# Second norm of a hybrid encoder layer: its weight moved to ScalarE behind the store, its 1/rms applied four row blocks at a time

## The chip, the cores and the metric

The kernel runs on one core of one Trainium2 chip. The metric is the device time of one execution in microseconds (us), as a median over runs. Engines are named as the profile names them: PE (TensorE matmul), PEld (its weight loads), DVE (VectorE), ACT (ScalarE), POOL (GpSimd) and SP (SyncE, which issues the DMAs). A name with a q, as SPq, is an engine's instruction queue.

## What is computed

One layer of an encoder, for 1024 frames of a new stream and 64 frames of a running one, 1088 columns together, with 1024 features. The part that matters here lies between the mixer and the feed-forward network (FFN):

```python
def _rmsnorm(x, g):
    xf = x.astype(jnp.float32)
    y = xf * lax.rsqrt(jnp.mean(xf * xf, axis=-1, keepdims=True) + EPS)
    return (y * g.astype(jnp.float32)).astype(x.dtype)

    mix = jnp.concatenate([y.astype(h.dtype), pool_out.astype(h.dtype)], axis=-1) @ w_out
    h = h + _rmsnorm(mix, post_mix_g)
    hn = _rmsnorm(h, pre_ffn_g)
    f = (jax.nn.silu(hn @ w_gate) * (hn @ w_up)) @ w_down
    h = h + _rmsnorm(f, post_ffn_g)
```

The third line is the first norm with its residual, the fourth is the second norm, with the weight `pre_ffn_g`. The value `h` of the third line is needed again in the last one, so the kernel stores it.

## The kernel before

Features lie on the 128 partitions, columns on the free axis. The 1088 columns are four chunks of 272, and the 1024 features are eight row blocks of 128, so an activation of a chunk is eight blocks of 128x272. Two tiles of four row blocks each (`mixf` for kh = 0 and 1, 128x1088) hold the mixer's output of a chunk. Products are made from high and low parts in three matmuls: ScalarE rounds a tile to its high part (`form`, a CAST, L1477) and VectorE subtracts it from the tile for the low part (`sub`, L416). Pool and VectorE additions that may disturb each other are marked "E" in the planner.

Every piece of work is a generator that yields which engine it wants and how long the planner assumes it to take; a planner (`Layout`) runs these generators against assumed times for all engines and so writes down, once, the instruction order of every engine. On the chip each engine runs its own list in order and waits on semaphores, so a late instruction holds back everything behind it in its list. All DMAs are issued from SP, in order.

`post_mix(c)` handles a chunk after the product with `w_out`. The column sums of squares of the mixer's output (name m0 to m3 for the chunks) go through `rstd_job`: PE sums over the partitions (L527, eight matmuls of one column in the trace), VectorE makes 1/rms in nine small operations (tile `t_m`, L532 to L561), PE transposes and spreads it into a PSUM bank (L565). Then `two(i)` handles four pairs of row blocks: VectorE multiplies the pair by 1/rms (L1422), Pool adds the residual `x` (L1431, `XM` names the engine per pair), the sum is the new `h`. After two pairs, four row blocks of `h` are stored with one DMA of 544 KB (`h_dram`). `SumSq` squares the pair on ScalarE (L617), sums the squares on VectorE (L624, L635) and starts the second norm (names h0 to h3): again `rstd_job` with its matmuls on PE, tile `t_h`, and then `norm(m)` for each of eight row blocks: one SCALAR_TENSOR_TENSOR on VectorE (L1457) that multiplies by the weight column and by 1/rms.

The FFN runs per pair of chunks, p = 0 for chunks 0 and 1, p = 1 for chunks 2 and 3. It uses seven products of combined operands, as Strassen's scheme does. `hforms(p)` makes the operands from the normed tiles: forms B11 and B21 from the first chunk alone, T1 to T4 from differences (L1489) and B22. A form is ready when its high part (ACT L1477) and its low part (DVE L416) are. The products of p = 0 are the first work of the FFN on PE; those of p = 1 follow while its last forms are still being made. A product's result can also wait for a partial sum in PSUM that VectorE has to take first (L1685, flag "x1").

Beside this, `w_pp` products (L492, a projection used much later) fill PE while the statistics of chunks 2 and 3 are worked out; ScalarE copies each result out of PSUM (tile `e`, L1825). At the start of the kernel, sums of squares of the input's first chunk are added by Pool (`XE`, tile `acc_x`, L772).

Of the kernel before, what the change touches and what calls it, by code (L numbers as in the profile page):

```python
# [14 lines left out]
P = 128  # L15
# [16 lines left out]
SEQ_IN = '4567pppp'  # L32
NZ = 3

XM, XF, XP = 'GGGG', 'GDGD', 'GDDD'
XE = ('AG', 'AD', 'AD', 'AD')

XL = 'GPGD'
NWARM, LW = 5, 256
# [16 lines left out]
P_DT = 3  # L56
P_DTE = 1
P_DTC = 4

FAST_M, FAST_H = (3,), (3,)  # L60

# [6 lines left out]
NK = 8  # L68
# [147 lines left out]
class Layout:  # L216
# [20 lines left out]
    def spawn(self, gen, prio=5):  # L237
        self.seq += 1
        job = {"gen": gen, "prio": (prio, self.seq), "t": max(self.now, self.done), "eng": "P", "req": None, "ready": 0.0}
        if self.step(job):  # L240
            self.jobs.append(job)
            self.jobs.sort(key=lambda j: j["prio"])
# [93 lines left out]
def trunk(ctx, tc, xT, par, wmix, wdt, poolw, wout, wff, wdn, wpg, wpp, pT, ssm0,  # L336
# [55 lines left out]
    def dma(dst, src, cols):  # L392
        sy.dma_start(dst, src)
        return lay.load(cols)
# [9 lines left out]
    def pcol(name, i=None, n=1):  # L404
        a, b = _PCOLS[name]
        if i is None:
            return cp[:, a:b]
        return cp[:, a + i:a + i + n]
# [996 lines left out]
    def post_mix(c, mf, ss):  # L1405

        L = CH[c][1]
        flag = []
        used = [0]
        added = [0, 0]  # L1410
        ss2 = SumSq(f"h{c}", 4, lambda: spawn(second(), 0), P_SQH)

        def two(i):
            if XM[i] != "A":
                yield n2.ok
                xr = n2.take(f"xr{c}_{i}")
                yield ("S", 0, 0)
                at = dma(xr, xT[c][:, 2 * i:2 * i + 2], 2 * L)
            yield lambda: bool(flag)
            v = mf[i // 2][:, i % 2 * 2:i % 2 * 2 + 2, :]  # L1420
            yield ("D", 0.72, 0)
            ve.tensor_tensor(v, v, flag[0][:, :L].unsqueeze(1).broadcast_to([P, 2, L]), ALU.mult)  # L1422
            used[0] += 1
            if used[0] == 4:
                banks.give(flag[0])
            if XM[i] == "A":
                yield ("S", 0, 0)
                yield ("S", 0, dma_add(v, xT[c][:, 2 * i:2 * i + 2], 2 * L))
            elif XM[i] == "G":
                yield ("G", 1.35, at)  # L1430
                gp.tensor_tensor(v, v, xr, ALU.add)  # L1431
            else:
                yield ("E", 0.73, at)
                ve.tensor_tensor(v, v, xr, ALU.add)
            if XM[i] != "A":
                n2.give(xr)
            added[i // 2] += 1
            if added[i // 2] == 2:
                dma(h1_d[c][:, i // 2 * 4:i // 2 * 4 + 4], mf[i // 2], 4 * L)
            ss2.add(v)  # L1440

        for i in range(4):
            spawn(two(i), 0)
        yield from rstd_job(ss.halves(), L, 1024.0, f"m{c}", flag, fast=c in FAST_M, free=ss.free)

        def second():
            got = []
            yield from rstd_job(ss2.halves(), L, 1024.0, f"h{c}", got, fast=c in FAST_H, free=ss2.free)
            r2 = got[0]
            left = [NK, 4, 4]  # L1450
            for m in range(NK):
                spawn(norm(m, r2, left), 0)

        def norm(m, r2, left):
            v = mf[m // 4][:, m % 4, :]
            yield ("D", 0.49, 0)
            ve.scalar_tensor_tensor(v, v, pcol("pre_ffn_g", m), r2[:, :L], ALU.mult, ALU.mult)  # L1457
            left[0] -= 1
            left[1 + m // 4] -= 1
            if not left[1 + m // 4]:  # L1460
                normed.add((c, m // 4))
            if not left[0]:
                banks.give(r2)

# [907 lines left out]
```

## Time and profile before

| | us |
|---|---|
| median of 3 runs | 1226.35 (1225.46 to 1226.62) |
| the profiled execution, its own time | 1227.99 |
| span in that profile | 1226.2 |
| PE busy in the span | 1201.8 (98%) |
| VectorE busy | 862.6 (70%) |
| ScalarE busy | 577.0 (47%) |
| GpSimd busy | 65.2 (5%) |

The profile is one execution taken by the hardware profiler. Busy time is an average over stages: the stage of this change covers about 315 to 424 us of the span. "Idle before" in a row names how long the engine had stood idle and what released it. PEclk, or the granted clock, is TensorE's clock as a share of its full 2.4 GHz.

### The profile page before, as it was taken

Reading aid. Unit: us, or ns where it says so; the run is one execution under the profiler, and the core shown is the slowest. Engines: PE = TensorE matmul, PEld = TensorE weight load, DVE = VectorE, ACT = ScalarE, POOL = GpSimd, SP = SyncE. Lnnn points to the kernel's source line nnn. Section 1 sums busy time; section 2 is a strip of 40 time slices with the busy share of each in tenths; the row PEclk is TensorE's granted clock in tenths of the full one; section 3 lists DMA queues with packets and bytes.
Section 4 is the critical chain, followed back from the end, with each engine's and each line's share of the span. In section 5 each row is a group of like instructions: output and inputs, shape, how many; then the busy total and the mean of one; then the engine's idle time right before and its main releaser. Section 6 shows DMA issues by size and latency. Waiting matters only on the chain.

```text
span 1226.2 us, 23743 instructions
## 1 busy us (share of the span) xinstructions
PE 1201.8 (98%) x9641; PEld 1181.8 (96%) x9641; DVE 862.6 (70%) x1572; ACT 577.0 (47%) x1123; POOL 65.2 (5%) x56
## 2 busy tenths in 40 slices
PE   8999999999999899999999999999999999999997
PEld 6999999999999899999999999999999999988996
DVE  5796867775798786776667667766746556688765
ACT  6354657964457444443444444443432212346543
POOL 2000000111241000000000000000000000002011
PEclk8999999999999899999999999999999999999998
DMA  6122122143446044444344334337978676334422
GB/s 226 42 74 80 62 96 92 52 133 114 135 161 225 14 137 148 153 153 133 134 162 145 130 138 163 132 122 263 404 280 291 213 254 231 115 96 132 142 74 83
DMA packets 73201, 182.01 MB, mean 148 GB/s; under 512 B 8636, under 2 KB 16644, under 8 KB 73092
## 3 DMA queue, kind: packets, MB, share of 16 engines
q1 hardware_dynamic: 73092, 180.50, 42.7%
q8 instruction: 75, 1.23, 0.4%
q14 instruction: 34, 0.28, 0.1%
HBM read 121.75 MB, written 58.72 MB: 147 GB/s over the span
## 4 chain that ended last, share of the span: by engine, by line
PE 92%; DVE 3%; ACT 2%; DMA 1%; issue 1%; SPq 0%; DVEq 0%; ACTq 0%
PE psall L1642 55%; PE psall L492 29%; PE psall L509 2%; PE psall L527 1%; PE psall L1128 1%; PE psall L565 1%; PE psall L1157 1%; PE psall L1122 1%; DVE f L1905 0%; DMA raw_in<-in_wmix_dram 0%; PE psall L1243 0%; PE psall L736 0%; DMA raw_out<-in_wout_dram 0%; DVE w_out L416 0%; DMA raw_pg<-in_wpg_dram 0%
## 5 line engine op out<-in xcount | busy, mean ns | idle before, releaser
L492 PE MATMUL psall<-x,w_in 128*128 128x272 f32 x1440 | 193.7, 291 | 0.0
L492 PEld LDWEIGHTS psall<-x,w_in 128*128 128x128 f32 x1440 | 184.0, 188 | 3.3 <-issue 2.8
L1905 DVE TENSOR_TENSOR f<-f,psall 128x544 f32<-128x544 f32 (+1 forms) x96 | 60.4, 636 | 68.8 <-PE psall L1642 67.0
L1642 PE MATMUL psall<-h_T,w_g_S 128*128 128x272 f32 x792 | 104.4, 292 | 3.2 <-DVE h_T L416 2.9
L1642 PEld LDWEIGHTS psall<-h_T,w_g_S 128*128 128x128 f32 x792 | 102.5, 193 | 3.6 <-DVE h_T L416 3.1
L1642 PE MATMUL psall<-al_T,w_d_S 128*128 128x272 f32 x768 | 100.4, 289 | 1.4 <-DVE f L1905 0.9
L1642 PE MATMUL psall<-h_T,w_u_S 128*128 128x272 f32 x792 | 100.8, 287 | 0.0
L1642 PEld LDWEIGHTS psall<-al_T,w_d_S 128*128 128x128 f32 x768 | 97.7, 188 | 2.3 <-ACT w_pg L463 0.9
L1642 PEld LDWEIGHTS psall<-h_T,w_u_S 128*128 128x128 f32 x792 | 99.6, 188 | 0.0
L492 PE MATMUL psall<-mix,w_out 128*128 128x272 f32 x720 | 93.5, 289 | 0.0
L492 PEld LDWEIGHTS psall<-mix,w_out 128*128 128x128 f32 x720 | 90.9, 188 | 0.0
L1642 PE MATMUL psall<-al_B,w_d_A 128*128 128x272 f32 x528 | 72.3, 289 | 2.7 <-DVE w_d_A L416 2.6
L492 PE MATMUL psall<-h,w_pg 128*128 128x272 f32 x576 | 74.7, 289 | 0.0
L492 PEld LDWEIGHTS psall<-h,w_pg 128*128 128x128 f32 x576 | 72.8, 188 | 0.0
L1642 PEld LDWEIGHTS psall<-al_B,w_d_A 128*128 128x128 f32 x528 | 68.5, 188 | 3.3 <-DVE w_d_A L416 3.1
L1642 PE MATMUL psall<-h_B,w_g_A 128*128 128x272 f32 x528 | 69.9, 288 | 0.0
L1642 PE MATMUL psall<-h_B,w_u_A 128*128 128x272 f32 x528 | 69.8, 288 | 0.0
L1642 PEld LDWEIGHTS psall<-h_B,w_u_A 128*128 128x128 f32 x528 | 67.7, 188 | 0.0
L1642 PEld LDWEIGHTS psall<-h_B,w_g_A 128*128 128x128 f32 x528 | 67.6, 188 | 0.0
L1570 ACT CAST w_d_A<-raw_d 128x512 fp32r<-128x512 f32 (+3 forms) x44 | 22.3, 522 | 70.2 <-PE psall L1642 35.1
L1570 ACT CAST w_d_S<-raw_d 128x512 fp32r<-128x512 f32 (+3 forms) x54 | 26.5, 532 | 56.4 <-DVE raw_d L1594 33.8
L416 DVE TENSOR_TENSOR w_u_S<-raw_u,w_u_S 128x512 fp32r<-128x512 f32 x44 | 30.3, 688 | 26.5 <-ACT w_u_S L1570 26.4
(407 smaller groups left out, 2211.7 us busy)
## 6 DMA issues: line engine op xcount, KB each, us to landing
af_dram<-a_T SPq DMA_DIRECT2D x88, 272.0 KB, 2.2
al_T<-af_dram SPq DMA_DIRECT2D x44, 544.0 KB, 6.1
af_dram<-a_B SPq DMA_DIRECT2D x66, 272.0 KB, 2.7
al_B<-af_dram SPq DMA_DIRECT2D x33, 544.0 KB, 6.4
raw_g<-in_wff_dram SPq DMA_DIRECT2D x22, 512.0 KB, 3.8
raw_u<-in_wff_dram SPq DMA_DIRECT2D x22, 512.0 KB, 3.7
raw_in<-in_wmix_dram SPq DMA_DIRECT2D x15, 512.0 KB, 3.8
raw_d<-in_wdn_dram SPq DMA_DIRECT2D x14, 512.0 KB, 4.6
```

Source lines behind the costliest of these rows:

```text
L416: eng.tensor_tensor(lo, src, hi.bitcast(F32), ALU.subtract)
L492: pe.matmul(out, lhsT, rhs, start=i == 0, stop=i == n - 1)
L509: pe.matmul(out, w.v(wi, k), act.v(xi, k, L), start=first and n == 0, stop=not left and n == 2)
L527: pe.matmul(ps[:n, 500 + 4 * i + j:501 + 4 * i + j], acc[:, n * j:n * j + n], ones[:, 0:1], start=True, stop=True)
L565: pe.transpose(pss[i][:, n * j:n * j + n], y[:, 4 * i + j:4 * i + j + 1].broadcast_to([n, P]), ident[:n, :n])
L1122: pe.matmul(py[:L, 256 * g:256 * g + 256], ct[:, g, t0:t0 + L], state[:, 256 * g:256 * g + 256], start=True, stop=True)
L1128: pe.matmul(pst[:, 256 * g:256 * g + 256], bk[:L, 128 * g:128 * g + 128], xw[:L, 4 * g:4 * g + 4].rearrange("p h q -> p (h q)"), start=Tru ...
L1157: pe.matmul(pyt[64 * r:64 * r + 64, P * b:P * b + L], xdt[:L, h], es[h // 4][:L, h % 4, :L], start=first, stop=True, skip_group_check=True)
L1570: ac.copy(v[:, 0], src)
L1642: pe.matmul(d[:, p - q.ps[0], :], w.v(wi, k), u.b(bf, xi, p, k), start=start and not k and not wi and not xi, stop=k == u.ks - 1 and wi == ...
L1905: ve.tensor_tensor(v[:, sl], v[:, sl], src[:, pl], ALU.add)
```

## The change

Four things change. (1) The weight is no longer part of `norm`: after a pair of row blocks has been stored and squared, ScalarE multiplies it in place by its weight column (new `scale`, two activations of 128x272 per pair). It must wait for the store, which reads the same rows, to have landed. (2) `norm` handles four row blocks at once with one TENSOR_TENSOR of 128x1088, whose second operand is the 1/rms in PSUM, read four times. It waits until both pairs of its tile are scaled. (3) `h` is stored per pair, in 16 DMAs of 272 KB, where there were 8 of 544 KB. (4) Two tables move additions from Pool to VectorE: the fourth pair's residual (`XM`) and the first chunk's sums of squares at the start (`XE`).

```diff
@@ -32,8 +32,8 @@
 SEQ_IN = '4567pppp'
 NZ = 3
 
-XM, XF, XP = 'GGGG', 'GDGD', 'GDDD'
-XE = ('AG', 'AD', 'AD', 'AD')
+XM, XF, XP = 'GGGD', 'GDGD', 'GDDD'
+XE = ('AD', 'AD', 'AD', 'AD')
 
 XL = 'GPGD'
 NWARM, LW = 5, 256
@@ -56,6 +56,7 @@
 P_DT = 3
 P_DTE = 1
 P_DTC = 4
+P_SCL = 0
 
 FAST_M, FAST_H = (3,), (3,)
 
@@ -1407,7 +1408,7 @@
         L = CH[c][1]
         flag = []
         used = [0]
-        added = [0, 0]
+        scaled = [0, 0]
         ss2 = SumSq(f"h{c}", 4, lambda: spawn(second(), 0), P_SQH)
 
         def two(i):
@@ -1434,10 +1435,15 @@
                 ve.tensor_tensor(v, v, xr, ALU.add)
             if XM[i] != "A":
                 n2.give(xr)
-            added[i // 2] += 1
-            if added[i // 2] == 2:
-                dma(h1_d[c][:, i // 2 * 4:i // 2 * 4 + 4], mf[i // 2], 4 * L)
-            ss2.add(v)
+            at = dma(h1_d[c][:, 2 * i:2 * i + 2], v, 2 * L)
+            ss2.add(v, lambda: spawn(scale(i, v, at), P_SCL))
+
+        def scale(i, v, at):
+
+            for q in range(2):
+                yield ("A", 0.48, at)
+                ac.activation(v[:, q], v[:, q], AF.Identity, scale=pcol("pre_ffn_g", 2 * i + q))
+            scaled[i // 2] += 1
 
         for i in range(4):
             spawn(two(i), 0)
@@ -1447,18 +1453,16 @@
             got = []
             yield from rstd_job(ss2.halves(), L, 1024.0, f"h{c}", got, fast=c in FAST_H, free=ss2.free)
             r2 = got[0]
-            left = [NK, 4, 4]
-            for m in range(NK):
-                spawn(norm(m, r2, left), 0)
-
-        def norm(m, r2, left):
-            v = mf[m // 4][:, m % 4, :]
-            yield ("D", 0.49, 0)
-            ve.scalar_tensor_tensor(v, v, pcol("pre_ffn_g", m), r2[:, :L], ALU.mult, ALU.mult)
+            left = [2]
+            for h in range(2):
+                spawn(norm(h, r2, left), 0)
+
+        def norm(h, r2, left):
+            yield lambda: scaled[h] == 2
+            yield ("D", 1.27, 0)
+            ve.tensor_tensor(mf[h], mf[h], r2[:, :L].unsqueeze(1).broadcast_to([P, 4, L]), ALU.mult)
             left[0] -= 1
-            left[1 + m // 4] -= 1
-            if not left[1 + m // 4]:
-                normed.add((c, m // 4))
+            normed.add((c, h))
             if not left[0]:
                 banks.give(r2)
```

Line numbers of the changed kernel are one higher from L59 on and four to six higher behind `post_mix`: L1457 becomes L1463, L1489 L1493, L416 L417, L527 L528, L1685 L1689, L1825 L1829; the new activation is L1445. Tile names carry running numbers that differ between the kernels.

VectorE's list behind the last 1/rms of chunk 3 (`t_h`), before; `mixf_0_3521` and `mixf_1_3522` are the halves of chunk 3, `h_T_1` rows make low parts of T forms, L1685 raises the flag x1:

```order
L561 SCALAR_TENSOR_TENSOR t_h_4837<-t_h_4837 68x4
L1457 SCALAR_TENSOR_TENSOR mixf_0_3521<-mixf_0_3521,cp,psall 128x272 x4
L1489 TENSOR_TENSOR mixf_0_3519<-mixf_0_3521,mixf_0_3519 128x1088
L1457 SCALAR_TENSOR_TENSOR mixf_1_3522<-mixf_1_3522,cp,psall 128x272 x4
L1685 TENSOR_TENSOR xr_2_3903<-xr_2_3903,psall 128x272
L416 TENSOR_TENSOR h_T_1_4913<-mixf_0_3519,h_T_0_4912 128x1088
L1489 TENSOR_TENSOR mixf_0_3519<-mixf_1_3522,mixf_0_3519 128x1088
L1693 TENSOR_TENSOR sq_m_3536<-sq_m_3536,psall 128x272
L1693 TENSOR_TENSOR p_3811<-p_3811,psall 128x272
L416 TENSOR_TENSOR w_u_A_4917<-raw_u_1_4655,w_u_A_4917 128x512
L1489 TENSOR_TENSOR mixf_0_3521<-mixf_1_3522,mixf_0_3521 128x1088
L416 TENSOR_TENSOR h_T_1_4952<-mixf_0_3519,h_T_0_4951 128x1088
```

The same place after:

```order
L1463 TENSOR_TENSOR mixf_0_3521<-mixf_0_3521,psall 128x1088
L1493 TENSOR_TENSOR mixf_0_3519<-mixf_0_3521,mixf_0_3519 128x1088
L1463 TENSOR_TENSOR mixf_1_3522<-mixf_1_3522,psall 128x1088
L417 TENSOR_TENSOR w_u_A_4836<-raw_u_0_4828,w_u_A_4836 128x512
L417 TENSOR_TENSOR h_T_1_4898<-mixf_0_3519,h_T_0_4897 128x1088
L1493 TENSOR_TENSOR mixf_0_3519<-mixf_1_3522,mixf_0_3519 128x1088
L1689 TENSOR_TENSOR p_3813<-p_3813,psall 128x272
L417 TENSOR_TENSOR w_u_A_4903<-raw_u_0_4828,w_u_A_4903 128x512
L417 TENSOR_TENSOR w_u_A_4911<-raw_u_1_4829,w_u_A_4911 128x512
L1493 TENSOR_TENSOR mixf_0_3521<-mixf_1_3522,mixf_0_3521 128x1088
L417 TENSOR_TENSOR h_T_1_4948<-mixf_0_3519,h_T_0_4947 128x1088
```

Two instructions stand in the place of eight, and the flag (L1689) now stands behind the low part of T1, the difference for T2 and one weight's low part.

ScalarE's list while the squares of chunk 3 are made, before; `e` copies free PSUM banks of the `w_pp` products, L617 squares the four pairs:

```order
L617 ACTIVATE p_3811<-mixf_0_3521 128x544
L1825 COPY e_7_4709<-psall 128x272
L1825 COPY e_0_4718<-psall 128x272
L617 ACTIVATE sq_m_3273<-mixf_0_3521 128x544
L1477 CAST h_B_0_4734<-mixf_0_3519 128x1088
L617 ACTIVATE sq_m_3273<-mixf_1_3522 128x544
L1825 COPY e_1_4732<-psall 128x272
L1477 CAST h_B_0_4766<-mixf_1_3520 128x1088
L1825 COPY e_2_4743<-psall 128x272
L617 ACTIVATE xr_2_3903<-mixf_1_3522 128x544
```

After:

```order
L618 ACTIVATE sq_m_3536<-mixf_0_3521 128x544
L1829 COPY e_6_4716<-psall 128x272
L1829 COPY e_7_4725<-psall 128x272
L618 ACTIVATE sq_m_3273<-mixf_0_3521 128x544
L1829 COPY e_0_4737<-psall 128x272
L1445 ACTIVATE mixf_0_3521<-mixf_0_3521,cp 128x272 x2
L618 ACTIVATE xr_2_3681<-mixf_1_3522 128x544
L1445 ACTIVATE mixf_0_3521<-mixf_0_3521,cp 128x272 x2
L618 ACTIVATE xr_2_3681<-mixf_1_3522 128x544
L1829 COPY e_1_4748<-psall 128x272
L1829 COPY e_2_4758<-psall 128x272
L1445 ACTIVATE mixf_1_3522<-mixf_1_3522,cp 128x272 x2
```

The scales of the first two pairs now stand between the squares of the last two, and the copies `e_1` and `e_2` behind both.

PE's list around the statistics of h2, before (`w_pp0` and `w_pp1` are the two halves of the weight; this is the second pass over `w_pp0`):

```order
L492 MATMUL psall_72<-p0_0_3802,w_pp0_3806 128x272 x2
L492 MATMUL psall_72<-p0_1_3805,w_pp0_3806 128x272
L527 MATMUL psall_72<-cp_73,p0_3811 68x1 x4
L492 MATMUL psall_72<-p0_1_3805,w_pp0_3806 128x272
L492 MATMUL psall_72<-p0_0_3802,w_pp0_3807 128x272 x2
```

After, in the first pass over `w_pp1`:

```order
L493 MATMUL psall_72<-p0_0_3804,w_pp0_3809 128x272 x2
L493 MATMUL psall_72<-p0_0_3804,w_pp1_3810 128x272 x2
L493 MATMUL psall_72<-p0_1_3807,w_pp1_3810 128x272
L528 MATMUL psall_72<-cp_73,sq_m0_3273 68x1 x4
L493 MATMUL psall_72<-p0_1_3807,w_pp1_3810 128x272
L493 MATMUL psall_72<-p0_0_3804,w_pp1_3811 128x272 x2
```

The statistics of h2 come after 27 matmuls of `w_pp`, where they came after 69. In the same way the statistics of h3 come after 18 matmuls of the FFN, where they came after 33, and the transposes of `t_h` of chunk 3 after 36, where they came after 57. The transposes of `t_m` of chunk 2 stand 12 matmuls earlier than before, those of chunk 3 15 matmuls earlier.

## Rows read from the trace of the kernel before

**Rows 1.** Page, busy time, share of the span and instructions of each engine.

```profile
PE 1201.8 (98%) x9641; PEld 1181.8 (96%) x9641; DVE 862.6 (70%) x1572; ACT 577.0 (47%) x1123; POOL 65.2 (5%) x56
```

**Rows 2.** Busy time by stretch, with PEclk, DMA share and GB/s at the end.

```profile
360.00:380.00 20.00, 20.00 (x166) 20.00 (x165) 19.86 (x21) 13.84 (x26) 7.71 (x4) 1.00 0.48 173
...
408.00:414.00 6.00, 3.68 (x25) 3.26 (x25) 5.39 (x10) 3.17 (x6) 0.00 (x0) 1.00 0.00 0
414.00:416.00 2.00, 0.00 (x0) 0.00 (x0) 2.00 (x2) 0.78 (x1) 0.00 (x0) 0.88 0.00 0
416.00:424.00 8.00, 7.56 (x39) 7.56 (x40) 5.88 (x6) 2.94 (x5) 0.00 (x0) 0.60 0.00 0
```

**Rows 3.** Timeline of PE, 396 to 424: start, duration, operation, count, idle before.

```profile
396.27 3.18 PE L1642 MATMUL psall<-h_B,w_g_A 128*128 128x272 f32 x24
...
400.41 0.60 PE L527 MATMUL psall<-cp,p 128*68 128x1 f32 x8
...
403.96 0.40 PE L565 MATMUL psall<-cp,t_h 68*128 68x68 f32 x4
...
409.54 1.79 PE L1642 MATMUL psall<-h_B,w_g_S 128*128 128x272 f32 x12 [1.74 <-DVE xr L1685]
...
413.20 0.39 PE L1642 MATMUL psall<-h_T,w_g_S 128*128 128x272 f32 x1 [0.37 <-ACT h_T L1477]
416.44 7.29 PE L1642 MATMUL psall<-h_T,w_g_S 128*128 128x272 f32 x35 [2.85 <-DVE h_T L416]
```

**Rows 4.** Timeline of DVE, 396 to 424, from the last 1/rms on.

```profile
404.46 1.72 DVE L1457 SCALAR_TENSOR_TENSOR mixf<-mixf,cp,psall 128x272 f32<-128x272 f32 x4 [1.23 <-PE psall L565]
406.22 1.29 DVE L1489 TENSOR_TENSOR mixf<-mixf,mixf 128x1088 f32<-128x1088 f32 x1
407.43 1.72 DVE L1457 SCALAR_TENSOR_TENSOR mixf<-mixf,cp,psall 128x272 f32<-128x272 f32 x4
409.06 0.43 DVE L1685 TENSOR_TENSOR xr<-xr,psall 128x272 f32<-128x272 f32 x1
409.41 1.28 DVE L416 TENSOR_TENSOR h_T<-mixf,h_T 128x1088 fp32r<-128x1088 f32 x1
...
413.30 0.69 DVE L416 TENSOR_TENSOR w_u_A<-raw_u,w_u_A 128x512 fp32r<-128x512 f32 x1
415.11 1.28 DVE L416 TENSOR_TENSOR h_T<-mixf,h_T 128x1088 fp32r<-128x1088 f32 x1
```

**Rows 5.** Instructions by line and form: count, duration in ns min/median/max.

```profile
L1422 DVE TENSOR_TENSOR mixf<-mixf,psall x16: 709/713/721, 315.9 to 390.2; 128x544 f32<-128x544 f32 x16
```

```profile
L1431 POOL TENSOR_TENSOR mixf<-mixf,xr x10: 1359/1378/2408, 319.4 to 393.1; 128x544 f32<-128x544 f32 x10
```

**Rows 6.** Timeline of ACT: eight activations of 128x272 in place with a weight column.

```profile
1097.49 3.40 ACT L2081 ACTIVATE f<-f,cp 128x272 f32<-128x272 f32 x8
```

**Rows 7.** DMA issues: bytes, median us from issue to landing.

```profile
h_dram<-mixf SPq DMA_DIRECT2D x8, 544.0 KB, 2.8
```

```profile
af_dram<-a_T SPq DMA_DIRECT2D x88, 272.0 KB, 2.2
```

**Rows 8.** Timelines of PE and DVE: the statistics of h2, and the last sum before.

```profile
379.13 0.60 PE L527 MATMUL psall<-cp,p 128*68 128x1 f32 x8
```

```profile
377.08 0.43 DVE L635 TENSOR_TENSOR p<-p 128x272 f32<-128x272 f32 x1
```

**Rows 9.** Timeline of DVE: the last sum before the statistics of h3.

```profile
398.83 0.43 DVE L635 TENSOR_TENSOR p<-p 128x272 f32<-128x272 f32 x1
```

**Rows 10.** Timelines of DVE and POOL: sums of squares beside residual additions.

```profile
318.46 3.34 DVE L624 TENSOR_TENSOR sq_m<-sq_m 128x544 f32<-128x544 f32 x2
```

```profile
319.36 3.67 POOL L1431 TENSOR_TENSOR mixf<-mixf,xr 128x544 f32<-128x544 f32 x2
```

**Rows 11.** Timelines of POOL and DVE at the start.

```profile
11.52 6.92 POOL L772 TENSOR_TENSOR acc_x<-acc_x,sqx 128x272 f32<-128x272 f32 x6 [0.45 <-ACT sqx L768]
```

```profile
14.62 0.34 DVE L858 TENSOR_TENSOR cp<-cp 128x4 f32<-128x4 f32 x1 [2.13 <-DMA cp<-in_par_dram]
```

## The prediction

> **What bounds the kernel now.** The page's table of busy time comes first: PE is busy for 1201.8 of 1226.2 us [rows 1], so only the 24.4 us in which it idles, and the time in which it runs below full speed, can be won by a change that takes no matmul away. This change takes none away. The table by stretch then shows where such time lies near the change. From 408 to 414 PE works 3.68 of 6 us, from 414 to 416 not at all, and from 416 to 424 it is busy again but at a granted clock of 0.60 [rows 2]. This is the beginning of the FFN.
>
> PE's timeline of that place names the waits: 1.74 us before the row at 409.54, on the sum for the flag x1 (VectorE L1685); 0.37 before 413.20, on the high part of T2; 2.85 before 416.44, on the low part of T2 (VectorE L416) [rows 3]. Together 4.96 us. The row at 396.27 has 24 matmuls in 3.18 us, 0.1325 each. The 35 matmuls from 416.44 would take 4.64 at that pace and took 7.29, so 2.65 us are lost to the clock, which fell while PE idled: 0.88 in the 2 us in which it does nothing, 0.60 behind that. The other two waits, of 1.74 and 0.37, left it at 1.00 [rows 2, 3]. The place costs 4.96 + 2.65 = **7.61 us**.
>
> VectorE's timeline says why the flag and T2 are late. It does not idle there: from 404.46 on it runs the second norm of chunk 3 in two runs of four, with a difference between them, then the flag's sum at 409.06, the low part of T1, and the low part of T2 at 415.11 [rows 4]. All of it hangs on the transposes of 1/rms at 403.96 [rows 3], and the first norm starts 0.50 after them. So two things decide: when the last 1/rms comes, and what VectorE runs between it and the two results.
>
> **The norm itself.** A run of four takes 404.46 to 406.22, 1.76 us; a 128x1088 subtraction from SBUF takes 1.29 alone, and starts 1.21 before its successor [rows 4]. The merged multiply, with its second operand in PSUM, is not in this trace. Below stands the 1.29 of that subtraction; above stand two 128x544 multiplies from PSUM, 2 x 0.713 = 1.43 [rows 5]. It is nearest to the 128x1088 subtraction, so I take 1.21 from start to start, which saves 0.55 per half and 1.1 on the way to T2 (0.7 at the other end).
>
> **The order behind it.** The transposes of the last 1/rms now come 21 matmuls earlier in the FFN, 21 x 0.1325 = 2.78 us: at 401.2 in the time of the trace of before, if the statistics are ready. Then, going down the new list of VectorE with the starts of [rows 4]: first half at 401.7, difference 402.9, second half 404.1, low part of a weight 405.3 (0.60 from 413.30 to 413.90, where the next subtraction begins; taken as 0.60), low part of T1 405.9, difference for T2 407.1, flag 408.3, done at 408.75. PE wants the flag at 409.54 - 1.74 = 407.80. It waits 0.95, where it waited 1.74, because the flag was moved behind three instructions. Then two weights (1.2), a difference (1.21), and the low part of T2 ends about 412.4. PE, which passes the flag 0.8 earlier, wants it at 413.20 - 0.37 - 0.8 + 0.39 = 412.4. So the 2.85 us wait goes, and with it, as no wait above 1.74 is left, the low clock. What is left is 0.95 of 7.61: a gain of **6.66**. With 1.43 for each multiply the flag waits 0.4 longer.
>
> **What the earlier statistics cost.** PE's list is in order, so a statistic that is put earlier and isn't ready stops everything behind it.
> - h2: its matmuls move 42 matmuls ahead, 5.57 us. The last sum before them ended at 377.51 and PE took them at 379.13, a slack of 1.62 [rows 8]. The sums must come 3.95 earlier. The transposes that start this chain are 12 matmuls earlier, 1.6. VectorE is busy for 19.86 of 20 us there, beside 7.71 of Pool [rows 2]; the change shortens a chunk's norm by 1.1 and adds one residual addition of some 0.72, a gain of 0.4. Two sums beside two Pool additions took 3.34, where such sums alone are about as long as the 0.713 of L1422, 1.43 [rows 5, 10]: each Pool addition costs VectorE about 0.95, and there is one fewer. 1.6 + 0.4 + 0.95 = 2.95, so PE waits 1.0. Ends: 0, and 2.35 if only the transposes come earlier.
> - h3: 15 matmuls, 2.0 us, against a slack of 400.41 - 399.26 = 1.15 [rows 3, 9], and its transposes are 15 matmuls earlier as well. One Pool addition (1.38 [rows 5]) leaves its chain; four scales in front of the last square enter it, 4 x 0.43 (eight take 3.40 [rows 6]) = 1.7. I put 0.3, with ends 0 and 2.0 (all of the shift lost).
>
> **The scales and stores.** 32 scales at 0.43 add 13.6 us to ScalarE, which has 6.16 idle in 360 to 380 [rows 2]. Each first waits for its store to land. The nearest rows are 2.8 us for 544 KB and 2.2 for 272 KB [rows 7]; I take 2.2. Behind the waiting scale are the squares of later pairs and the `e` copies, on which PE's banks hang. The squares are in the line above; for the copies I put 0.3 (0 to 1.5). SP issues eight more stores, all in this stage: no engine but ScalarE waits for one before the norms do. The Trainium skill ("DMA: Bandwidth & Descriptors", section "Anatomy of one DMA — SWDGE (gpsimd) path") holds that about 2.0 us of a DMA are fixed, whatever its size; 2.2 against 2.8 for half the bytes agrees, though these are issued by SP. By its fit a 272 KB store takes some 2.6 us (an estimate), which would add 0.4 at most to the copies.
>
> **The start.** Seven additions go from Pool, where six took 6.92, to VectorE, at about the 0.43 of L1685: 3.0 us. VectorE idled 2.13 us before 14.62, waiting for a DMA that its new list no longer puts there [rows 4, 11]. I put 0, from -0.5 to +0.7.
>
> **Sum.** -6.66 + 1.0 + 0.3 + 0.3 = -5.06. From the profiled execution's 1227.99 that gives 1222.93; it lies 1.64 above the median of 1226.35, so the forecast is **1221.3**.
>
> **Rivals.**
> - *All is absorbed.* No new waits, the flag too in time: the whole 7.61, 1218.7. For it: the statistics' chains also lose a Pool addition. Against it: the flag's own walk leaves 0.95.
> - *The second result stays late.* The last 1/rms comes only 0.7 earlier instead of 2.78: then the flag waits about as before, T2 about 1.3 to 2, and the clock falls again. What remains is 0.55 per half, 1.1, less 1.0 for h2: 1226.3. For it: VectorE's list is in order and the flag now stands three instructions deeper.
> - *The store's landing becomes the bound.* SP's list is in order; a store behind a load that still waits for its buffer is issued late, and the scale then holds ScalarE, its squares and the copies. With all the upper ends, 2.35 + 2.0 + 1.5 = 5.85, and one of these waits as long as the 2.85 that came before the low clock, another 2.65: -6.66 + 5.85 + 2.65 = +1.84, 1228.2, slower by 0.15%; with the second result late as well, +1.84 + 2.85 = +4.7, 1231. It decides from a landing of about 4 us on.
> - *Pool and VectorE block each other.* Two sums beside two Pool additions took 3.34 [rows 10], and the moved fourth addition now runs beside Pool's third. If it waits for all of it, 1.38 more in the chains of h2 and h3, 2.1 together after h3's slack: 1223.4. The Trainium skill ("SBUF — State Buffer", section "Who interferes with whom") says that a VectorE instruction with two SBUF inputs and a GpSimd one that reads SBUF exclude each other for a whole instruction. The 3.34 is between no blocking (1.43) and two whole waits (4.2), so the trace bears it out in part.
>
> **Chances.** 0.45 for the forecast, 0.08 for all absorbed, 0.12 for the blocking, 0.18 for a late second result, 0.17 for the landing. A measurement of this kernel tells about 0.2%, 2.45 us, from no change: faster is below 1223.9, slower above 1228.8. The first three are faster, but for some of the blocking (0.62); the second result late is the same, with that rest and a quarter of the landing (0.25); the rest of the landing is slower (0.13). The range reaches from the first rival to where the landing begins, 1218.5 to 1228.2.
>
> **What would show it.** In the profile after: the transposes of the last 1/rms 36 matmuls into the FFN; no PE wait above 1.5 us from 400 to 425, and a granted clock of 1.00 throughout; a merged norm of 1.2 to 1.45; PE waits on VectorE at the statistics of h2 of about 1; store landings of 2.0 to 2.8. The forecast is wrong if ScalarE waits on DMAs while PE waits on ScalarE between 315 and 400, or if a wait of over 2 us before T2 is left.

## The result: 0.6% faster

The changed kernel takes 1220.20 us, median of 5 runs (1219.06 to 1222.34), where the kernel before, run beside it on the same chip, took 1226.62 (1225.46 to 1230.02). The ratio is 0.9943, with a 95% interval from 0.9924 to 0.9962. The forecast was 1221.3 in a range from 1218.5 to 1228.2. The profiled execution after took 1222.34 us with a span of 1220.6; before, 1227.99 and 1226.2. The spans differ by 5.6 us, and that is the difference that can be looked up in the two traces.

Busy time hardly moved, as the page after shows (engine, busy us, share, instructions); PE's answers to [rows 1]:

```profile
PE 1199.7 (98%) x9641; PEld 1180.5 (97%) x9641; DVE 862.8 (71%) x1559; ACT 587.8 (48%) x1155; POOL 51.0 (4%) x45
```

VectorE's total is what it was (862.6 before): it runs the 11 additions that Pool lost and a shorter norm. The gain is in PE's waits. PE's timeline after at the beginning of the FFN, which answers to [rows 3]:

```profile
402.08 0.40 PE L566 MATMUL psall<-cp,t_h 68*128 68x68 f32 x4
...
409.92 1.77 PE L1646 MATMUL psall<-h_B,w_g_S 128*128 128x272 f32 x12 [1.36 <-DVE p L1689]
411.53 1.67 PE L1646 MATMUL psall<-h_B,w_g_A 128*128 128x272 f32 x12
413.04 0.29 PE L1646 MATMUL psall<-h_T,w_g_S 128*128 128x272 f32 x1
413.53 4.74 PE L1646 MATMUL psall<-h_T,w_g_S 128*128 128x272 f32 x35 [0.20 <-DVE h_T L417]
```

The waits of 1.74, 0.37 and 2.85 have become 1.36, nothing and 0.20, and the 35 matmuls that took 7.29 take 4.74. The table by stretch after (columns as in [rows 2], granted clock third from the end) has the clock at 1.00 in every stretch, also where it was 0.88 and 0.60:

```profile
360.00:380.00 20.00, 20.00 (x165) 20.00 (x165) 19.69 (x29) 17.95 (x37) 3.51 (x2) 1.00 0.48 165
...
408.00:414.00 6.00, 4.43 (x33) 3.99 (x32) 5.96 (x8) 2.93 (x4) 0.00 (x0) 1.00 0.00 0
414.00:416.00 2.00, 2.00 (x18) 2.00 (x17) 2.00 (x4) 0.78 (x2) 0.00 (x0) 1.00 0.00 0
416.00:424.00 8.00, 8.00 (x65) 7.97 (x64) 5.64 (x8) 4.85 (x10) 0.00 (x0) 1.00 0.01 2
```

One stretch serves as a ruler below: from the transposes of m0, where the two orders still agree, to the first matmul with `w_u`, behind the waits. Its two ends on PE, before and after:

```profile
315.49 0.40 PE L565 MATMUL psall<-cp,t_m 68*128 68x68 f32 x4
...
423.57 1.68 PE L1642 MATMUL psall<-h_B,w_u_A 128*128 128x272 f32 x12
```

```profile
315.54 0.40 PE L566 MATMUL psall<-cp,t_m 68*128 68x68 f32 x4
...
418.11 2.18 PE L1646 MATMUL psall<-h_B,w_u_A 128*128 128x272 f32 x16
```

The stretch fell from 108.08 to 102.57, by 5.51 us: the whole difference of the spans. It splits at the end of the last wait. Up to there PE gained 416.44 - 413.53 + 0.05 = 2.96, behind it 7.13 - 4.58 = 2.55, the low clock.

VectorE's timeline after shows the way to T2; it answers to [rows 4]:

```profile
402.58 1.29 DVE L1463 TENSOR_TENSOR mixf<-mixf,psall 128x1088 f32<-128x1088 f32 x1 [0.43 <-PE psall L566]
403.90 1.29 DVE L1493 TENSOR_TENSOR mixf<-mixf,mixf 128x1088 f32<-128x1088 f32 x1
405.11 1.28 DVE L1463 TENSOR_TENSOR mixf<-mixf,psall 128x1088 f32<-128x1088 f32 x1
406.31 0.69 DVE L417 TENSOR_TENSOR w_u_A<-raw_u,w_u_A 128x512 fp32r<-128x512 f32 x1
406.91 1.29 DVE L417 TENSOR_TENSOR h_T<-mixf,h_T 128x1088 fp32r<-128x1088 f32 x1
408.23 1.29 DVE L1493 TENSOR_TENSOR mixf<-mixf,mixf 128x1088 f32<-128x1088 f32 x1
409.44 0.43 DVE L1689 TENSOR_TENSOR p<-p,psall 128x272 f32<-128x272 f32 x1
...
412.19 1.29 DVE L417 TENSOR_TENSOR h_T<-mixf,h_T 128x1088 fp32r<-128x1088 f32 x1
```

From the transposes to the end of the low part of T2 it took 416.39 - 403.96 = 12.43 us before and takes 413.48 - 402.08 = 11.40 now. The transposes come 402.08 - 397.01 = 5.07 after the first FFN matmul, where they came 403.96 - 396.27 = 7.69 after it. So T2 is 2.62 earlier by its place and 1.03 by its length. Against this the FFN itself begins 0.69 later on the ruler, because the projection before it is longer; that leaves the 2.96.

Before, a sum that stood ahead of T2 in VectorE's list waited for PE itself, by VectorE's timeline of the kernel before:

```profile
412.94 0.44 DVE L1693 TENSOR_TENSOR p<-p,psall 128x272 f32<-128x272 f32 x1 [0.58 <-PE psall L1642]
```

After, VectorE waits for nothing between the transposes' result and the end of T2.

### The profile page after: what moved, and what is told of

It is laid out like the page before. It is cut to its first block, busy times and chain, and to the rows that moved or that the text cites. A ratio compares the mean times of both kernels' runs of the same rounds, so it can differ in the third digit from the quotient of the medians.

```text
span 1220.6 us, 23782 instructions
## 1 busy us (share of the span) xinstructions
PE 1199.7 (98%) x9641; PEld 1180.5 (97%) x9641; DVE 862.8 (71%) x1559; ACT 587.8 (48%) x1155; POOL 51.0 (4%) x45
## 4 chain that ended last, share of the span: by engine, by line
PE 91%; DVE 3%; DMA 2%; ACT 2%; issue 1%; SPq 0%; ACTq 0%; DVEq 0%
PE psall L1646 54%; PE psall L493 29%; PE psall L510 3%; PE psall L528 1%; DMA al_B<-af_dram 1%; PE psall L566 1%; PE psall L1129 1%; PE psall L1158 1%; PE psall L1123 1%; DMA raw_d<-in_wdn_dram 0%; PE psall L737 0%; PE psall L1244 0%; DVE f L1909 0%; DMA raw_in<-in_wmix_dram 0%; DMA raw_out<-in_wout_dram 0%
## 5 line engine op out<-in xcount | busy, mean ns | idle before, releaser
L1646 PE MATMUL psall<-h_T,w_g_S 128*128 128x272 f32 x792 | 101.7, 288 | 0.2 <-DVE h_T L417 0.2
L1646 PEld LDWEIGHTS psall<-h_T,w_g_S 128*128 128x128 f32 x792 | 100.0, 188 | 0.5 <-DVE h_T L417 0.4
L417 DVE TENSOR_TENSOR w_u_S<-raw_u,w_u_S 128x512 fp32r<-128x512 f32 x44 | 30.2, 687 | 26.8 <-ACT w_u_S L1574 26.8
```

The lines of the kernel that those rows point to most:

```text
L417: eng.tensor_tensor(lo, src, hi.bitcast(F32), ALU.subtract)
L1646: pe.matmul(d[:, p - q.ps[0], :], w.v(wi, k), u.b(bf, xi, p, k), start=start and not k and not wi and not xi, stop=k == u.ks - 1 and wi == ...
```

## The experiments

The theory: the gain is the gap at the FFN's start, by the place of the last 1/rms in PE's list and by what VectorE runs behind it; the low clock goes as soon as no long wait is left. The rivals were that the merged multiply, Pool's relief, the start, the stores or ScalarE behind the stores decides. Each run is judged by its ratio to the kernel before, timed beside it, and by the ruler in its own profile, which does not depend on when the input arrives. "Gap" is the time from the first FFN matmul to the first with `w_u`, "projection" the time from the first `w_pp` matmul to the first of the FFN.

| kernel | ratio (95% interval) | ruler | projection | gap |
|---|---|---|---|---|
| before | 1 | 108.08 | 25.71 | 27.30 |
| after | 0.9943 (0.9924 to 0.9962) | 102.57 | 26.40 | 21.10 |
| fourth_only | 0.9982 (0.9972 to 0.9991) | 105.51 | 25.84 | 24.64 |
| scale_only | 0.9974 (0.9963 to 0.9985) | 105.17 | 25.61 | 24.53 |
| store_pairs | 0.9988 (0.9979 to 0.9998) | 108.20 | 26.00 | 27.15 |
| start_only | 0.9984 (0.9974 to 0.9993) | 106.95 | 25.68 | 26.19 |
| start_back | 0.9945 (0.9928 to 0.9961) | 102.57 | 26.40 | 21.10 |
| unmerged | 0.9945 (0.9930 to 0.9960) | 101.87 | 27.13 | 19.69 |
| fourth_back | 0.9945 (0.9930 to 0.9960) | 103.69 | 29.36 | 19.32 |
| no_weight | 0.9944 (0.9929 to 0.9959) | 102.04 | 26.44 | 20.57 |
| plan_short | 0.9991 (0.9982 to 1.0001) | 106.87 | 26.94 | 24.85 |
| plan_long | 0.9975 (0.9965 to 0.9985) | 106.19 | 26.33 | 24.78 |
| after_two_adds | 0.9957 (0.9942 to 0.9972) | 103.82 | 28.47 | 20.25 |
| after_unmerged_two_adds | 0.9937 (0.9922 to 0.9952) | 102.75 | 28.06 | 19.25 |

### The order alone

**plan_long**, the kernel after with one assumed time changed:

```diff
-            yield ("D", 1.27, 0)
+            yield ("D", 1.96, 0)
             ve.tensor_tensor(mf[h], mf[h], r2[:, :L].unsqueeze(1).broadcast_to([P, 4, L]), ALU.mult)
```

> The kernel after, instruction for instruction, with only the planner's assumed time for a merged multiply raised from 1.27 to 1.96, so that the order alone changes: the last transposes of 1/rms after 42 matmuls of the FFN instead of 36 (0.8 us later). From the transposes of m0 to the first matmul with w_u the kernel after takes 102.6 us, the one before 108.1. Theory (the place of the last 1/rms sets the low part of T2): about 103.3 with the clock kept; if one wait exceeds 2, the low clock too, 104.8. Rival (the shorter instructions are the gain, whatever the order): 102.6.

Measured: ratio 0.9975, ruler 106.19. With the same instructions more than half of the gain is gone, further than expected. PE's timeline in this kernel:

```profile
413.85 6.18 PE L1646 MATMUL psall<-h_T,w_g_S 128*128 128x272 f32 x35 [3.48 <-DVE h_T L417]
```

The flag is in time, but T2 is 3.48 late. VectorE's timeline in this kernel says why: the flag's sum comes early (405.70), and then, ahead of the low part of T2, stands a sum that waits for PE.

```profile
405.70 0.43 DVE L1689 TENSOR_TENSOR sq_m<-sq_m,psall 128x272 f32<-128x272 f32 x1
...
410.35 0.44 DVE L1697 TENSOR_TENSOR sq_m<-sq_m,psall 128x272 f32<-128x272 f32 x1 [1.14 <-PE psall L1646]
410.71 0.69 DVE L417 TENSOR_TENSOR w_u_A<-raw_u,w_u_A 128x512 fp32r<-128x512 f32 x1
411.31 1.28 DVE L1493 TENSOR_TENSOR mixf<-mixf,mixf 128x1088 f32<-128x1088 f32 x1
412.51 1.28 DVE L417 TENSOR_TENSOR h_T<-mixf,h_T 128x1088 fp32r<-128x1088 f32 x1
```

Against the kernel after, T2 ends 2.24 later, counted from the first FFN matmul: 1.32 because the transposes come later (6.39 instead of 5.07 behind it; six matmuls, and a wait of 0.41 on ScalarE among them), and 0.92 because the way from the transposes to T2 is longer (12.32 instead of 11.40). PE, which no longer waits for the flag, comes to T2 1.03 earlier, and so waits the longer. So the order counts for more than the length of the instructions, and not only by the place of the last 1/rms: it also counts whether VectorE's list has something in front of T2 that waits for PE. In the kernel after, the two sums of L1697 stand behind the low part of T2.

**plan_short**, the reverse, on the kernel before:

```diff
-            yield ("D", 0.49, 0)
+            yield ("D", 0.32, 0)
             ve.scalar_tensor_tensor(v, v, pcol("pre_ffn_g", m), r2[:, :L], ALU.mult, ALU.mult)
```

> The kernel before, instruction for instruction, with only the planner's assumed time for one norm multiply cut from 0.49 to 0.32, so that the order alone changes (last transposes 6 matmuls earlier, 0.8 us). Theory: waits 4.96 - 0.8, above 2 in one piece, the low clock stays: 1225 to 1226.6. Rival, that a reordering of any sort closes the gap: 1221 to 1223.

Measured: 0.9991, not to be told from no change, with waits of 0.98, 0.38 and 2.18 in the gap and the low clock behind the last. The waits fell by 1.4, more than the 0.8 expected; a reordering of any sort does not close the gap.

### The parts alone

**scale_only**, the kernel before with the weight on ScalarE and the stores per pair; the norm is still eight multiplies:

```diff
-XM, XF, XP = 'GGGD', 'GDGD', 'GDDD'
-XE = ('AD', 'AD', 'AD', 'AD')
+XM, XF, XP = 'GGGG', 'GDGD', 'GDDD'
+XE = ('AG', 'AD', 'AD', 'AD')
...
-            ve.tensor_tensor(mf[h], mf[h], r2[:, :L].unsqueeze(1).broadcast_to([P, 4, L]), ALU.mult)
+            for m in range(4):
+                yield ("D", 0.43, 0)
+                ve.tensor_tensor(mf[h][:, m], mf[h][:, m], r2[:, :L], ALU.mult)
```

(against the kernel after)

> The kernel before with the weight moved to ScalarE and the stores per pair, and nothing else: eight multiplies of 128x272 by 1/rms, all four residual additions on Pool, Pool's additions at the start. The planner puts the last transposes of 1/rms after 42 matmuls of the FFN (57 before, 36 after). Theory (place of the last 1/rms, length of what VectorE has to run behind it): of the 4.96 us of waits at the start of the FFN some 2.5 go, no single wait over 2, the clock stays up: 5 of 7.6 won there, 0.5 to 1 lost in the projection before: 1221 to 1223. Rival (the merged multiply is what matters): 1225 to 1226.6.

**fourth_only**, the kernel before with the fourth addition on VectorE:

```diff
-XM, XF, XP = 'GGGG', 'GDGD', 'GDDD'
+XM, XF, XP = 'GGGD', 'GDGD', 'GDDD'
```

> The kernel before with one edit: the fourth pair's residual addition on VectorE. The norm stays eight multiplies, the stores stay 544 KB. The planner then puts the last transposes of 1/rms 13 matmuls of the FFN earlier (1.7 us; the full change moves them 21, 2.78 us). Theory, that the gain is the gap at the start of the FFN, by the place of the last 1/rms and the norm's length: the waits there fall from 4.96 to about 3.3, the clock may or may not fall: 1222 with the clock kept, 1225 with it lost. Rival, that taking additions off Pool is what counts: nearly the whole gain, 1221.

Each of the two alone wins about half: the ruler falls by 2.9 and 2.6. In both the flag's wait is nearly gone, and one wait before T2 is left, with the low clock behind it. PE's timeline of scale_only, then of fourth_only:

```profile
413.91 6.18 PE L1647 MATMUL psall<-h_T,w_g_S 128*128 128x272 f32 x35 [2.67 <-DVE h_T L417]
```

```profile
414.12 6.19 PE L1642 MATMUL psall<-h_T,w_g_S 128*128 128x272 f32 x35 [2.77 <-DVE h_T L416]
```

For scale_only the expectation of no single wait above 2 and of 1221 to 1223 was wrong (1223.91); it also has a wait of 0.73 at the statistics of h3. Neither part alone keeps the clock up. The scales with the moved addition do (unmerged, below), and so do the scales with the merged multiply (fourth_back).

**store_pairs**, the kernel before with 16 stores instead of 8:

```diff
-            added[i // 2] += 1
-            if added[i // 2] == 2:
-                dma(h1_d[c][:, i // 2 * 4:i // 2 * 4 + 4], mf[i // 2], 4 * L)
+            dma(h1_d[c][:, 2 * i:2 * i + 2], v, 2 * L)
```

> The kernel before with 16 stores of 272 KB instead of 8 of 544, and nothing else. The last transposes stay after 57 matmuls. Theory: worth nothing, 108 us from the transposes of m0 to the first matmul with w_u, 1226 to 1227. Rival (earlier landings let the norms start earlier): 1225 or less.

Ruler 108.20, the waits in the gap as before (1.68, 0.37, 2.84). Its time was 1.1 us below that of the kernel before, at the edge of its interval, and its profile has nothing for that: no gain in this place.

**start_only** and **start_back**, the start's additions alone and undone:

```diff
-XE = ('AG', 'AD', 'AD', 'AD')
+XE = ('AD', 'AD', 'AD', 'AD')
```

> The kernel before with only the first chunk's sums of squares moved to VectorE. Theory: 1226 to 1227, the gap at the start of the FFN unchanged at 27.3 us from the first FFN matmul to the first with w_u. Rival: 2 us faster, 1224.6.

> The kernel after with the first chunk's sums of squares back on Pool. The order from the first norm's transposes on is the same. Theory: the start is worth nothing at the end, since VectorE's later work sets the mixer's end: 1220 to 1221, and the stretch from the first projection matmul on as after. Rival (the earlier first statistics, 19.89 against 21.95 us, are worth 2 us): 1222.

start_only leaves the waits of before as they are; this is PE's timeline at the flag and at T2:

```profile
407.51 1.77 PE L1642 MATMUL psall<-h_B,w_g_S 128*128 128x272 f32 x12 [1.74 <-DVE xr L1685]
...
414.39 6.20 PE L1642 MATMUL psall<-h_T,w_g_S 128*128 128x272 f32 x35 [2.83 <-DVE h_T L416]
```

Still its ratio is 0.9984, a gain of some 2 us, nearer to the rival's than to none. 1.1 of the ruler is a shorter spell of low clock (6.20 where the profiled execution of the kernel before has 7.29, behind the same waits). start_back on the other hand loses nothing against the kernel after (0.9945 and 0.9943). Over the fourteen profiles the transposes of m0 come at 314.2 to 315.5 in the six kernels with Pool's additions, on average 314.8, and at 312.3 to 315.5 in the eight with VectorE's, on average 313.8. That is 1.0 us for the start with a scatter as large; in the profile of the kernel after there is none of it (315.54). Whether the start is worth 0 or 1 us is open.

### What is needed of the rest

**unmerged**, the kernel after with the merged multiply taken apart:

```diff
-            yield ("D", 1.27, 0)
-            ve.tensor_tensor(mf[h], mf[h], r2[:, :L].unsqueeze(1).broadcast_to([P, 4, L]), ALU.mult)
+            for m in range(4):
+                yield ("D", 0.43, 0)
+                ve.tensor_tensor(mf[h][:, m], mf[h][:, m], r2[:, :L], ALU.mult)
```

> The kernel after, but each half's merged multiply is four multiplies of 128x272 by 1/rms in PSUM; the weight stays with ScalarE. The last transposes come after 27 matmuls. Theory: each half costs 1.5 to 1.7 us instead of 1.2, the flag x1 and T2 move by 0.6 to 1.0, but the earlier transposes pay for it: 1220 to 1222, granted clock 1.00. Rival, that the merging itself is the gain: the waits of before return, 1224 to 1226.

Measured: 0.9945, as fast as the kernel after. VectorE's timeline here:

```profile
400.87 1.48 DVE L1464 TENSOR_TENSOR mixf<-mixf,psall 128x272 f32<-128x272 f32 x4
...
403.60 1.48 DVE L1464 TENSOR_TENSOR mixf<-mixf,psall 128x272 f32<-128x272 f32 x4
```

Four multiplies take 1.48, one merged 1.28: merging is worth 0.2 per half, and the earlier place of the last 1/rms outweighs it. The multiply that takes no weight is 0.37 each, where that with a weight was 0.43 [rows 4]. The transposes come 3.93 after the first FFN matmul here, 5.07 in the kernel after. The rival that merging is the gain falls: where the fourth addition is moved too, merging is not needed.

**fourth_back**, the kernel after with the fourth addition on Pool again:

```diff
-XM, XF, XP = 'GGGD', 'GDGD', 'GDDD'
+XM, XF, XP = 'GGGG', 'GDGD', 'GDDD'
```

> The kernel after with the fourth addition back on Pool (as before the change); merged norm, scales and stores per pair stay. The planner puts the last transposes even earlier, after 27 matmuls of the FFN. Theory (place of the last 1/rms and length of the norm): the gap stays closed, if the sums are ready; PE waits up to 1 us at the statistics of chunk 3: 1219.5 to 1221.5. Rival (Pool's additions are what counts): most of the gain goes, 1224 to 1226.

Pool has its residual additions back and the ratio stays (0.9945), so Pool's relief is not the gain either. Beside scale_only, which has neither, the moved addition (unmerged) and the merged multiply (fourth_back) each bring the gap from 24.53 to under 20: with the scales one of the two is enough, and by the ratio it does not matter which. Both kernels also have the start's additions on VectorE, which alone leave the waits in the gap as they are (start_only). The gap is closed altogether (19.32, no wait in it), and the projection in front of it is 3.65 longer than before, with waits of 1.8 on copies and 1.0 on a merged multiply, none at the statistics where they were expected. PE's timeline there, and ScalarE's around it:

```profile
371.94 3.23 PE L493 MATMUL psall<-p,w_pp 128*128 128x272 f32 x24 [1.49 <-ACT e L1829]
```

```profile
368.93 0.94 ACT L1445 ACTIVATE mixf<-mixf,cp 128x272 f32<-128x272 f32 x2
369.76 0.85 ACT L1522 ACTIVATE mixf<-psall,cp 128x272 f32<-128x272 f32 x2
370.50 1.10 ACT L1481 CAST h_T<-mixf 128x1088 fp32r<-128x1088 f32 x1
371.49 1.25 ACT L1829 COPY e<-psall 128x272 f32<-128x272 f32 x4
```

ScalarE is busy without a break behind its scales and casts, and the copies that free PE's banks come late. The trace suggests that this is what the new work on ScalarE can cost; no run took the scales out of this kernel. It is not the stores' landing: neither here nor in the kernel after does ScalarE stand idle before a scale.

**no_weight**, the kernel after without the scales, so that the second norm's weight is missing from its result:

```diff
-                yield ("A", 0.48, at)
-                ac.activation(v[:, q], v[:, q], AF.Identity, scale=pcol("pre_ffn_g", 2 * i + q))
+                yield ("A", 0.0, at)
```

> The kernel after without the 32 scales on ScalarE; the weight of the second norm is left out of the computation. PE's order is nearly the same as after. Measures what the scales and their wait for the store cost. Theory: only the 0.7 us by which the projection before the FFN got longer, on ScalarE's copies: 1219.5 to 1220.2. Rival (ScalarE behind the store's landing is the hidden bound): 1217 to 1218.5.

Measured: 0.9944, the projection as long as after (26.44). The 0.5 on the ruler is the flag's wait, 0.82 instead of 1.36. So 32 scales cost half a microsecond by the ruler and nothing that the ratio shows, and the 0.7 by which the projection grew is not theirs, against the expectation. Some of it is in PE's timeline of the kernel after, at a copy that stands behind a CAST of `h_B` on ScalarE's list:

```profile
385.21 1.78 PE L493 MATMUL psall<-p,w_pp 128*128 128x272 f32 x12 [0.25 <-ACT e L1829]
```

```profile
383.77 1.10 ACT L1481 CAST h_B<-mixf 128x1088 fp32r<-128x1088 f32 x1
384.77 0.68 ACT L1829 COPY e<-psall 128x272 f32<-128x272 f32 x2
```

### Trying for more

**after_two_adds** and **after_unmerged_two_adds** put the third pair's addition on VectorE as well (`XM = 'GGDD'`), the second of them with the multiply taken apart as above.

> The kernel after with the third pair's residual addition on VectorE as well. The last transposes come after 30 matmuls (36 after the change). Meant as a better version: Pool's chain shorter by 1.38 per chunk, VectorE's longer by 0.72. Theory: the flag and T2 0.8 earlier, 101.8 us from the transposes of m0 to the first matmul with w_u, 1219.5. Rival (VectorE, full from 360 to 380, becomes the bound and PE waits at the statistics of h2): 103.5, 1221.

> As the previous kernel (third and fourth addition on VectorE), with each merged multiply as four multiplies of 128x272, which in the unmerged kernel took 1.48 against 1.28 per half. The last transposes come after 21 matmuls. Unmerged alone took 101.9 us from the transposes of m0 to the first matmul with w_u. Theory: the gap at the FFN's start is closed, about 19.5 us long; the projection before it is stretched by ScalarE's copies: 101 to 102, 1219 to 1220. Rival: PE waits at the statistics of h3, which are put after 3 matmuls of the FFN: 103.5, 1221.

Both have a shorter gap than after (20.25 and 19.25) and a longer projection (28.47 and 28.06). In the first, this is the table of PE's waits from 315 to 424 (what waited for what, us in total, times, longest):

```profile
PE psall L493 <- ACT e L1829: 2.2, 2, 1.4
PE psall L1646 <- DVE sq_m L1689: 0.6, 1, 0.6
PE psall L1646 <- DVE h_T L417: 0.2, 1, 0.2
```

The rival's sum was right for the first, but not its cause: PE waits on ScalarE's copies, not at the statistics of h2, and the 101.8 that the theory gave is missed by 2. The second has its gap as expected, but a ruler of 102.75 where 101 to 102 was expected. It is the best ratio of all, 0.9937, but its interval holds the ratio of the kernel after: no version was shown to be better than the change.

These two kernels are also where a store's landing holds ScalarE, the rival of the prediction: it stands idle before a scale for 0.54 at 319.21 in the first, and for 0.23 at 318.07 and 1.53 at 342.88 in the second. PE's timeline names no wait from 315 to 371 in either, so nothing was seen to come of it.

## Why the prediction was right, point by point

**The bound and its price.** The 7.61 us at the FFN's start were the right place: 5.5 of them are what the traces differ by. Of the 2.65 put down to the clock 2.55 came back. That term is a property of one execution, though: behind last waits of 2.18 to 3.48 the same 35 matmuls took 6.18 to 6.20 in five other kernels, and 7.20 in store_pairs. With the usual 6.2 the loss is 1.5, so the sum leaned on a profile with a long spell.

**The norm.** 1.21 from start to start was taken for the merged multiply, 1.29 long; it is 1.28:

```profile
L1463 DVE TENSOR_TENSOR mixf<-mixf,psall x8: 1281/1284/1289, 338.7 to 405.1; 128x1088 f32<-128x1088 f32 x8
```

The operand in PSUM, read four times, costs nothing over one in SBUF.

**The order behind it.** The place of the last 1/rms was foreseen as 2.78 earlier and is 2.62. The pace was too long: 0.1325 is the length of a row divided by its count, but from one row's start to the next one's the same 24 matmuls of [rows 3] take 399.28 - 396.27 = 3.01, 0.125 each, and 21 x 0.125 = 2.62. The flag waits 1.36, not 0.95. Its sum starts 7.36 after the transposes instead of 7.1, because a difference that needs the result just in front of it starts 1.32 after that (402.58 to 403.90, 406.91 to 408.23) and not 1.21, and PE asks for it 0.1 sooner after the transposes. T2 waits 0.20, foreseen as none. No wait of 2 is left, and the clock stays, as foreseen.

**The statistics.** At h2 a wait of 1.0 was foreseen, and there is none. VectorE's and PE's timelines after, answering to [rows 8]:

```profile
372.12 0.44 DVE L636 TENSOR_TENSOR sq_m<-sq_m 128x272 f32<-128x272 f32 x1
```

```profile
373.94 0.60 PE L528 MATMUL psall<-cp,sq_m 128*68 128x1 f32 x8
```

The sums end at 372.56, 4.95 earlier than before; 2.95 were counted on. Fewer were needed than thought, too: PE takes the statistics 379.13 - 373.94 = 5.19 earlier, not 5.57, again the pace, so 3.57 instead of 3.95. Where the 4.95 come from can be read from PE's transposes of `t_m` of chunk 2 and from the last addition. The timelines of PE and Pool before, and of PE after:

```profile
358.61 0.40 PE L565 MATMUL psall<-cp,t_m 68*128 68x68 f32 x4
...
365.87 1.84 POOL L1431 TENSOR_TENSOR mixf<-mixf,sq_m 128x544 f32<-128x544 f32 x1
```

```profile
357.16 0.40 PE L566 MATMUL psall<-cp,t_m 68*128 68x68 f32 x4
```

The last addition ends at 365.87 + 1.84 = 367.71 on Pool before, and at 362.21 + 1.88 = 364.09 on VectorE after (shown below). The transposes come 1.45 earlier (1.6 was put). From them to the end of the last addition it took 9.10 and takes 6.93, 2.17 less; from there to the end of the sums 9.80 and 8.47, 1.33 less. For these two, 3.50 together, the prediction had 0.95 + 0.4 = 1.35. So the term that was mis-sized is the relief of the additions and the sums behind them. At h3 0.3 was put, and PE waits for none: the last sum ends at 397.77, PE takes it at 399.28.

**Scales and stores.** The landing of the 272 KB stores was 2.0 us, where 2.2 was taken:

```profile
h_dram<-mixf SPq DMA_DIRECT2D x16, 272.0 KB, 2.0
```

ScalarE never waited for one. The 2.6 that the fit in the Trainium skill ("DMA: Bandwidth & Descriptors", section "Anatomy of one DMA — SWDGE (gpsimd) path") gives was too long here. Nor do these stores bear out its fixed 2.0 us, as the prediction read them: 2.0 is the whole of the 272 KB store, and with 2.8 for twice the bytes about 1.2 is left for what does not grow with the size (an estimate from these two). The copies were put at 0.3; the projection grew by 0.7, of which the trace names 0.25 and the scales none.

**Pool against VectorE.** The moved addition takes 0.72 where Pool is done, and up to 1.88 beside it, as VectorE's timeline after shows:

```profile
341.05 0.72 DVE L1435 TENSOR_TENSOR mixf<-mixf,sq_m 128x544 f32<-128x544 f32 x1
...
360.13 2.16 DVE L1493 TENSOR_TENSOR mixf<-mixf,mixf 128x1088 f32<-128x1088 f32 x1
362.21 1.88 DVE L1435 TENSOR_TENSOR mixf<-mixf,xr 128x544 f32<-128x544 f32 x1
```

Pool's timeline beside it:

```profile
358.45 1.37 POOL L1432 TENSOR_TENSOR mixf<-mixf,p 128x544 f32<-128x544 f32 x1 [17.51 <-DVE mixf L1423]
359.78 3.73 POOL L1432 TENSOR_TENSOR mixf<-mixf,sq_m 128x544 f32<-128x544 f32 x2
```

Alone, a Pool addition takes 1.37, the difference 1.29 and the moved addition 0.72. From 359.78 on the times are those of whole instructions in turn: Pool's second addition to about 361.1, the difference to 362.29, Pool's third to 363.51, the moved addition to 364.09. So the moved addition waited through all of a Pool addition, which cost it 1.16 where the rival assumed 1.38. The 3.34 of [rows 10], which the prediction took for a blocking in part, fits whole turns as well: the first of the two sums came when a Pool addition was under way, the second waited through a whole one. This agrees with the Trainium skill ("SBUF — State Buffer", section "Who interferes with whom"), where a VectorE instruction with two SBUF inputs contends with a GpSimd instruction that reads SBUF, and the lock is exclusive. The rival had the mechanism, but no wait of PE from 315 to 424 was traced to it; what it cost is inside the 6.93 above.

**The sum.** Foreseen -5.06 in the profile, measured -5.6. The terms that failed partly cancelled: 1.3 put for h2 and h3 did not come, and about 1.1 came that was not put (flag 0.4, T2 0.2, projection 0.4, clock 0.1); some 0.3 stay unassigned. That the forecast came so close is in that part luck. The medians differ by 6.4; the 0.8 beyond the profiles is within what the runs of one kernel scatter, and the start may hold part of it.

## What to carry to other kernels

In a kernel whose engines run fixed lists, an edit that makes one stage's work a little shorter can be worth more by what the planner then writes than by the work itself: the same instructions under another order lost more than half of this gain. Before costing an edit, read the new order at the place where the bound engine waits, and walk down the list that it waits for, instruction by instruction, with durations of the trace; look above all for an instruction in that list that itself waits for the bound engine. And a wait behind which the clock falls costs more than its length: the 2.77 us in fourth_only cost 1.45 more.

## What the runs showed of the hardware

TensorE's granted clock stayed at 1.00 (2.4 GHz) behind waits of 1.36 and 1.74 us, and fell to 0.50 (1.2 GHz) during or behind every last wait of 2.18 us and more in this place. Shorter waits lay in front of most of these, so no run shows what of the idle time decides. What a fall costs is not a constant: 35 matmuls that take 4.74 us at full clock took 6.18 to 6.20 in five kernels and 7.20 and 7.29 in two. start_only (6.20) and the kernel before (7.29) stand on the two sides with the same waits in front (1.74, 0.4, 2.8).

A VectorE multiply of 128x1088 whose second operand is one bank of PSUM, read four times by its access pattern, takes 1.28 us, as long as one with both operands in SBUF; four of 128x272 take 1.48 together.

VectorE instructions with both operands in SBUF and Pool additions took turns by whole instructions: a VectorE addition of 0.72 us took 1.88 beside Pool, and two Pool additions 3.73 where two take 2.69 undisturbed (at 341.05 in the kernel before). The multiplies of L1422, with one operand in PSUM, took 0.709 to 0.721 in all 16 [rows 5], some of them beside Pool additions.
